# An encoder layer on one core: the two interleaved threads resume by counted TensorE time, and dense pieces hold six products

## The chip, the cores and the metric

The kernel runs on one core of a Trainium2 chip. The metric is the device time of one execution in microseconds (us). A core has a matrix engine (TensorE, PE in the rows, with its weight loads as PEld), three further engines (VectorE or DVE, ScalarE or ACT, GpSimd or POOL) and a DMA queue that SyncE (SP) issues. Each engine takes its own instructions in order and waits on semaphores for the others.

## The reference

One encoder layer over 2048 tokens of width 1024 in fp32. Three mixers run beside each other, then an output projection and a gated feed-forward layer.

```
h = rms_norm(x, norm_mix);  p = h @ w_in          # split by columns
out_a = dsa_mixer(...)   # per block of 128 queries: score all keys, keep the 256 best of the
                         # admissible ones, softmax over those, sum of latent values
out_b = gla_mixer(...)   # gated linear attention in chunks of 64, with a carried state
out_c = swa_mixer(...)   # attention in a window of 128 with sinks
x = x + concat(out_a, out_b, out_c) @ w_out
h = rms_norm(x, norm_ffn)
x = x + (silu(h @ w_ffn_gate) * (h @ w_ffn_up)) @ w_ffn_down
return rms_norm(x, final_norm)
```

## The kernel before, in words

A large product is done in fp32r as three matmuls of 512 columns for each 128 rows of the contraction (high by high, low by high, high by low halves of the operands); a weight tile that comes from memory for the first time is split into its halves on ACT (line 114) and POOL (line 117), and stored for later use.

The tokens stand in four groups of 512. The program is written by two Python generators that `merge` interleaves into one instruction stream.

- **dense** writes, for each group, `pass1` (the projections that the sparse mixer needs), then `pass2` (gated linear attention and window attention, each with their projections in `proj`), and then `ffn` for groups 0 and 1, one group at a time. The feed-forward products are lines 199 to 201 (gate and up, output projection) and 509 to 511 (down).
- **dsa** writes the sparse mixer for 16 blocks of 128 queries. `select` scores the keys (lines 1115 and 1116) and then finds the 256th best value by bisection: 8 and 23 rounds of `probe`, alternately on ACT (line 1153) and DVE (line 1155), each of which reads all keys of the block and is followed by two tiny DVE instructions that set the next threshold; then lines 1194 to 1208 make the mask, with a DVE scan (line 1203). `attend` runs for the block before, in an inner `merge` with `select`: for each head, `logits` (three matmuls, lines 1248 to 1250, for each strip of keys, reduced on DVE at line 1252, then Exp on ACT at line 1256), then for pairs of heads `turned` (four transposes at line 1265, a copy on ACT at line 1267) and `summed` (line 1275).

After each piece a generator yields its cost in us of work. `merge` divides what a thread has yielded by its total, and resumes the thread that is furthest behind. The total of dsa is multiplied by `SPEED`, 1.3; a larger number makes it count as further behind, so it is resumed earlier. `FINE`, 4, is the number of contraction tiles, of three matmuls each, after which `proj` and the feed-forward products yield, so dense comes in pieces of 12 matmuls. A thread that yields None (its input is not written yet) is passed over.

What the generators write is a program with an order of priority. The framework that builds the queues of the engines from it decides the final order on each of them, and adds all semaphores.

When both generators are at their end, `ffn` runs once more for groups 2 and 3 together (lines 352 to 354 and 509 to 511, PSUM tile `pf`). In that part one generator runs alone.

PSUM tiles for `dsa` are `sc` (2 buffers), `tr` (2, shared with dense) and `o` (1); those of dense are `mm` (2) or `mf` (3).

Of the kernel before, what the change touches and what calls it, by code (L numbers as in the profile page):

```python
# [40 lines left out]


def merge(*threads):


    live = []
    for gen, total in threads:
        live.append([0.0, float(max(total, 1e-9)), gen])
    while live:
        for t in sorted(live, key=lambda e: e[0] / e[1]):  # L50
            try:
                c = next(t[2])
            except StopIteration:
                live.remove(t)
                break
            if c is None:
                continue
            t[0] += c
            yield c
            break  # L60
        else:
            yield None

# [6 lines left out]
def drive(gen):  # L70
    for _ in gen:
        pass

SPEED = 1.3
FINE = 4

# [6 lines left out]
def hybrid_encoder_kernel(ctx, tc, xT, w_in, w_out, w_g, w_u, w_d, vec, wuk, wuv, wg2,  # L85
                          relb, cst, onehot, out):
    nc = tc.nc
    V, A, T, Q = nc.vector, nc.scalar, nc.tensor, nc.gpsimd

# [93 lines left out]
    def ffn(groups, pools, ps_f, ps_n, n_raw, n_w, n_act, n_lead, before, prepare=iter(())):  # L183
# [67 lines left out]
        def normed(i):  # L251

            hs = halves[i]
            norm_scale(hs)
            h2.append([])
            for k in range(KC):
                h2[i].append(operand(i, k))
                hi, lo = h2[i][k]
                hf = fr.tile([P, 512], F32, tag="m", bufs=n_m, name="hf")
                V.scalar_tensor_tensor(out=hf, in0=x2[:, k, hs], scalar=vc[:, V_FFN + k:V_FFN + k + 1],  # L260
                                       in1=rs[:, hs], op0=ALU.mult, op1=ALU.mult)
                A.copy(hi, hf)  # L262
                (V if k % 2 else Q).tensor_sub(lo, hf, hi.bitcast(F32))
                yield 0.4
# [302 lines left out]
    with ExitStack() as mx:  # L567
# [249 lines left out]
        def to_tokens(ps, dst):  # L817

            t = gen_tile("t")
            A.copy(t, ps)  # L820
            pt = ps_tr()
# [38 lines left out]
        def gla_qkv(j, h, bx, first=None):  # L860
            qe = gl.tile([P, 2, G], F32, tag="qe", name="qe")
            Q.memset(qe[64:128, 0, :], 0.0)
            Q.memset(qe[0:64, 1, :], 0.0)
            ke = gl.tile([P, G], F32, tag="ke", name="ke")
            kd = gl.tile([P, 4, P], F32, tag="kd", name="kd")
            vt = gl.tile([P, 2, 4, P], F32, tag="vt", name="vt")
            ps = first[0] if first else (yield from proj(CH_QB + j, h))
            for hh in range(2):
                r = slice(hh * 64, hh * 64 + 64)
                V.scalar_tensor_tensor(out=qe[r, hh, :], in0=ps[r], scalar=0.125, in1=bx["e1"][r],  # L870
                                       op0=ALU.mult, op1=ALU.mult)
            if not first:
                yield 5.2 - PART
            ps = first[1] if first else (yield from proj(CH_KB + j, h))
            db = bx["db"]
            V.tensor_mul(ke, ps, bx["e2"])
            V.tensor_mul(db, ps, db)
            pt = ps_tr()
            for t in range(4):
                T.transpose(pt[:, t * P:(t + 1) * P], db[:, t * P:(t + 1) * P], ident)  # L880
            A.copy(kd, pt.rearrange("p (b d) -> p b d", b=4))
            yield 5.7 - PART
            for hh in range(2):
                ps = yield from proj(CH_VB + 2 * j + hh, h)
                to_tokens(ps, vt[:, hh])
                yield 5.7 - PART
            bx.update(qe=qe, ke=ke, kd=kd, vt=vt)
# [15 lines left out]
        def gla_mix(g, j, bx):  # L903

            qe, ke, kd, vt, dec = (bx[n] for n in ("qe", "ke", "kd", "vt", "dec"))
            for t2 in range(2):
                pa = ps_mm()
                for u in range(2):
# [7 lines left out]
                                op=ALU.mult)  # L916
                yield 1.0

# [10 lines left out]
                for n in range(4):  # L929
# [12 lines left out]
                    S_st[j] = nw  # L942
                yield 1.8
                po = ps_ot()
# [14 lines left out]
                A.activation(sq, po, AF.Square)  # L959
                yield 1.8  # L960
                pm = ps_tr()
# [18 lines left out]
        def swa_qkv(g, h, bx):  # L980
            qc = gl.tile([P, 2, G], F32, tag="qc", name="qc")
            for i in range(2):
                ps = yield from proj(CH_QC + i, h)
                A.activation(qc[:, i, :], ps, AF.Copy, scale=0.125)
                yield 5.2 - PART
            ps = yield from proj(CH_KC, h)
            if g > 0:
                Q.tensor_copy(kct[:, 0:P], kct[:, G:G + P])
                Q.tensor_copy(vct[:, 0, :], vct[:, 4, :])
            V.tensor_copy(kct[:, P:], ps)  # L990
            yield 5.2 - PART
            ps = yield from proj(CH_VC, h)
            to_tokens(ps, vct[:, 1:5, :])
            bx["qc"] = qc
            yield 5.7 - PART

        def swa_mix(g, bx):
            qc = bx["qc"]
            for b in range(4):
# [4 lines left out]
                for kv in range(2):  # L1004
# [11 lines left out]
                    lg.append(l2)  # L1016
                yield 1.8
                den = sp.tile([P, 4], F32, tag="den", name="den")
# [10 lines left out]
                yield 1.0  # L1029
                kbs = [1] if k0 else [0, 1]  # L1030
                pts = {}
                for kb in kbs:
# [6 lines left out]
                    pts[kb] = pT  # L1039
                yield 1.2  # L1040
                po = ps_ot()
# [48 lines left out]
        def select(qb, res):  # L1090
# [18 lines left out]
            ql = selp.tile([P, 512], F32R, tag="ql", name="ql")  # L1109
            split(qf, qh, ql)  # L1110
            x = selp.tile([P, S], F32, tag="x", name="x")
            for k0, w in strips(nk):
                for hd in range(4):
                    ps = ps_sc()
                    T.matmul(ps[:, 0:w], qh[:, hd * P:(hd + 1) * P], ks[:, k0:k0 + w], start=True, stop=False)
                    T.matmul(ps[:, 0:w], ql[:, hd * P:(hd + 1) * P], ks[:, k0:k0 + w], start=False, stop=True)
                    wt = w_tok[:, qb, hd:hd + 1]
                    if hd == 0:
                        V.tensor_scalar(out=x[:, k0:k0 + w], in0=ps[:, 0:w], scalar1=0.0, scalar2=wt,
                                        op0=ALU.max, op1=ALU.mult)  # L1120
                    else:
                        r = sel_tile("r")
                        A.activation(r[:, 0:w], ps[:, 0:w], AF.Relu)
                        V.scalar_tensor_tensor(out=x[:, k0:k0 + w], in0=r[:, 0:w], scalar=wt,
                                               in1=x[:, k0:k0 + w], op0=ALU.mult, op1=ALU.add)
                yield 4 * w / 512.0
            Q.memset(x[0:64, nk - 64:nk], LOW)
# [32 lines left out]
            for i in range(8):  # L1160
# [4 lines left out]
                                op0=ALU.bitwise_or, op1=ALU.bitwise_xor)  # L1165
                yield nk / 980.0 + 0.6

# [6 lines left out]
            for k in range(1, 24):  # L1174
                lim, few, enough = probe(k % 2 == 1)
                if k < 23:
# [4 lines left out]
                                    op0=ALU.subtract, op1=ALU.add)  # L1181
                yield nk / 1000.0 + 0.6

# [7 lines left out]
            V.tensor_scalar(out=ntt, in0=ntt, scalar1=-1.0, scalar2=None, op0=ALU.mult)  # L1191
            yield nk / 960.0 + 0.8

# [15 lines left out]
            res.append(mk)  # L1209
            yield 4.0 * nk / 960.0  # L1210

# [6 lines left out]
        def attend(qb, res):  # L1218
# [3 lines left out]
            nc.sync.dma_start(out=qa[:, 0:256].rearrange("p (j t) -> p j t", j=2),  # L1222
                              in_=qaD[g].rearrange("j p t -> p j t")[:, :, q0:q0 + P])
            pq = ps_sc()
            for hd in range(4):
# [4 lines left out]
            A.activation(lh, pq, AF.Copy, scale=0.125)  # L1230
            V.scalar_tensor_tensor(out=ll, in0=pq, scalar=0.125, in1=lh.bitcast(F32), op0=ALU.mult, op1=ALU.subtract)
            x = res[0]
            nw = min(nk, 256)
# [5 lines left out]
            def logits(hd):  # L1239
# [5 lines left out]
                for si, (k0, w) in enumerate(sl):  # L1245
# [8 lines left out]
                                           op0=ALU.add, op1=ALU.min, accum_out=least[:, si:si + 1])  # L1254
                    yield 0.9 * w / 512.0
                A.activation(lg[:, 0:nk], lg[:, 0:nk], AF.Exp, scale=-1.0, bias=least[:, si:si + 1],
# [24 lines left out]
            for h2 in (0, 2):  # L1281
                yield from logits(h2)
                yield from logits(h2 + 1)
                for k4 in range(0, qb + 1, 4):
                    nxt = [turned(h2, k4)]
# [3 lines left out]
                    wait = nxt  # L1289
                    yield 2.0 * nxt[0][2] / 4.0  # L1290
            V.reciprocal(den, den)

            pt = ps_tr()
# [3 lines left out]
            summed(*wait)  # L1297
            pb = ps_tr()
            for hd in range(4):
# [167 lines left out]
```

## Time and profile before

| | us |
|---|---|
| median of 3 runs | 2904.71 (2903.05 to 2909.02) |
| the profiled execution, its own time | 2900.37 |
| its span, first to last instruction | 2898.6 |
| TensorE busy in the span | 2701.9 (93%) |
| VectorE busy | 1791.0 (62%) |
| ScalarE busy | 1251.7 (43%) |
| GpSimd busy | 837.1 (29%) |
| mean granted TensorE clock | 0.971 of full |

The span and the execution's own time differ by 1.8 us. Busy times overlap between engines, so they don't add up to the span; what matters is the idle time of the engine that sets the pace in a stage.

### The profile page before, as it was taken

To read this page: it belongs to the slowest core of one execution; us is meant where nothing else is said; L and a number is where in the kernel's file an instruction comes from. 1 tells how busy PE (TensorE), PEld (TensorE's weight loads), DVE (VectorE), ACT (ScalarE), POOL (GpSimd) and SP (SyncE) were. 2 spreads that over 40 slices of the span, in tenths; PEclk is the share of its full clock that TensorE was granted. 3 is DMA by queue.
4 is the path that set the end of the run, shared out by engine and by line. 5 is a ranking of instruction groups with operands and counts; after the bars stand their busy time and mean duration, and the time that the engine had idled before them with its cause. 6 is when DMAs were issued, how large, how long until landed. Compare 5 with 4: busy or idle time off the path is not lost. (4 is left out here: it accounts for less than half of the span.)

```text
span 2898.6 us, 37034 instructions
## 1 busy us (share of the span) xinstructions
PE 2701.9 (93%) x13108; PEld 2120.4 (73%) x13108; DVE 1791.0 (62%) x3661; ACT 1251.7 (43%) x2183; POOL 837.1 (29%) x681
## 2 busy tenths in 40 slices
PE   7898999999999989998988998999998999999997
PEld 5666767677776767776766777878776888888885
DVE  3887897787776767465477564464546544444446
ACT  4655664565555645354455342342433211111114
POOL 3113420010100454544443200000223444354443
PEclk9999999999999989999999999999999999999998
DMA  7565534243332756766667444435473443334432
GB/s 258 191 193 196 181 123 142 94 144 112 98 130 83 245 207 215 247 206 218 216 212 244 164 159 134 150 127 167 173 256 130 132 136 107 120 123 134 131 99 102
DMA packets 191113, 471.08 MB, mean 163 GB/s; under 512 B 19944, under 2 KB 51600, under 8 KB 190928
## 3 DMA queue, kind: packets, MB, share of 16 engines
q1 hardware_dynamic: 190928, 468.71, 48.8%
q8 instruction: 104, 1.70, 0.2%
q14 instruction: 81, 0.66, 0.1%
HBM read 341.61 MB, written 127.02 MB: 162 GB/s over the span
## 5 line engine op out<-in xcount | busy, mean ns | idle before, releaser
L117 POOL TENSOR_TENSOR w<-raw,w 128x512 fp32r<-128x512 f32 x272 | 366.9, 1360 | 592.5 <-ACT w L114 559.2
L1153 ACT ACTIVATE jd<-x,c 128x384 bf16<-128x384 f32 (+13 forms) x224 | 292.9, 1307 | 299.1 <-DVE c L1180 237.2
L199 PE MATMUL mf<-ah,w 128*128 128x512 f32 x832 | 333.1, 401 | 6.4 <-ACT ah L262 2.6
L201 PE MATMUL mf<-al,w 128*128 128x512 f32 x832 | 330.4, 398 | 7.8 <-DVE al L243 5.0
L1155 DVE TENSOR_SCALAR_CACHE_REDUCE jd<-x,c 128x384 bf16<-128x384 f32 (+13 forms) x224 | 330.9, 1477 | 6.9 <-DVE c L1164 0.5
L200 PE MATMUL mf<-ah,w 128*128 128x512 f32 x832 | 328.6, 396 | 0.0
L114 ACT CAST w<-raw 128x512 fp32r<-128x512 f32 x272 | 165.3, 617 | 364.3 <-PE pf L511 190.9
L354 PE MATMUL pf<-al,w 128*128 128x512 f32 x616 | 242.6, 394 | 7.4 <-DVE al L277 3.7
L352 PE MATMUL pf<-ah,w 128*128 128x512 f32 x616 | 242.4, 393 | 4.3 <-ACT ah L276 4.3
L724 PE MATMUL mm<-hh,w 128*128 128x512 f32 x576 | 240.2, 417 | 4.3 <-issue 2.0
L353 PE MATMUL pf<-ah,w 128*128 128x512 f32 x616 | 241.4, 392 | 0.0
L725 PE MATMUL mm<-hh,w 128*128 128x512 f32 x576 | 231.3, 402 | 0.0
L726 PE MATMUL mm<-hl,w 128*128 128x512 f32 x576 | 230.1, 400 | 0.0
L201 PEld LDWEIGHTS mf<-al,w 128*128 128x128 f32 x832 | 159.3, 192 | 45.0 <-DVE al L243 5.5
L199 PEld LDWEIGHTS mf<-ah,w 128*128 128x128 f32 x832 | 159.4, 192 | 40.9 <-issue 4.9
L512 DVE TENSOR_TENSOR x<-x,pf 128x512 f32<-128x512 f32 (+1 forms) x184 | 121.9, 663 | 106.1 <-PE pf L511 105.1
L200 PEld LDWEIGHTS mf<-ah,w 128*128 128x128 f32 x832 | 159.5, 192 | 32.1
L509 PE MATMUL mf<-fh,w 128*128 128x512 f32 x352 | 143.9, 409 | 17.2 <-ACT fh L114 6.9
L117 POOL TENSOR_TENSOR fl<-u,fh 128x512 fp32r<-128x512 f32 x44 | 58.0, 1319 | 320.9 <-ACT fh L114 320.9
L354 PEld LDWEIGHTS pf<-al,w 128*128 128x128 f32 x616 | 116.8, 190 | 35.3 <-DVE al L277 5.7
L510 PE MATMUL mf<-fh,w 128*128 128x512 f32 x352 | 141.4, 402 | 1.1 <-POOL w L117 1.1
L511 PE MATMUL pf<-fl,w 128*128 128x512 f32 (+1 forms) x368 | 141.2, 384 | 0.6 <-POOL fl L117 0.6
(296 smaller groups left out, 5921.9 us busy)
## 6 DMA issues: line engine op xcount, KB each, us to landing
w<-w SPq DMA_DIRECT2D x622, 512.0 KB, 3.6
raw<-in_w_g_dram SPq DMA_DIRECT2D x88, 256.0 KB, 3.6
raw<-in_w_u_dram SPq DMA_DIRECT2D x88, 256.0 KB, 3.5
xk<-in_xT_dram SPq DMA_DIRECT2D x64, 256.0 KB, 3.2
raw<-in_w_in_dram SPq DMA_DIRECT2D x44, 256.0 KB, 3.7
raw<-in_w_d_dram SPq DMA_DIRECT2D x44, 256.0 KB, 3.7
m<-mixT SPq DMA_DIRECT2D x32, 256.0 KB, 3.2
x<-in_xT_dram SPq DMA_DIRECT2D x32, 256.0 KB, 5.4
```

The costliest lines, as they stand in the source:

```text
L117: Q.tensor_sub(lo, src, hi.bitcast(F32))
L199: T.matmul(ps, a, act[k][0], start=(first and k == ks[0]), stop=False)
L200: T.matmul(ps, b, act[k][0], start=False, stop=False)
L201: T.matmul(ps, a, act[k][1], start=False, stop=(last and k == ks[-1]))
L352: T.matmul(ps, x, b[0], start=first, stop=False)
L353: T.matmul(ps, y, b[0], start=False, stop=False)
L354: T.matmul(ps, x, b[1], start=False, stop=last)
L724: T.matmul(ps, a, hh, start=(k == 0), stop=False)
L725: T.matmul(ps, b, hh, start=False, stop=False)
L726: T.matmul(ps, a, hl, start=False, stop=(k == KC - 1))
L1153: A.activation(jd, xs, AF.Sign, scale=-1.0, bias=c[:, 0:1], accum_out=cnt)
L1155: V.tensor_scalar(out=jd, in0=xs, scalar1=c[:, 0:1], scalar2=0.0, op0=ALU.is_ge, op1=ALU.add, accum_out=cnt)
```

## The change

`merge` gets a clock of its own, `now`, that `drive` advances by the TensorE time of each piece as it is written. A piece can now yield three numbers: its cost for the balance between the threads, its TensorE time, and a latency. After such a piece its thread isn't resumed until `now` has moved on by the latency; the other thread is written meanwhile. A yield of zero cost and zero TensorE time states a latency alone. When every thread waits, the shortest wait is handed up, and `drive` advances `now` by it without writing anything.

```
 def merge(*threads):
     live = []
     for gen, total in threads:
-        live.append([0.0, float(max(total, 1e-9)), gen])
+        live.append([0.0, float(max(total, 1e-9)), gen, 0.0])
     while live:
+        wait = None
         for t in sorted(live, key=lambda e: e[0] / e[1]):
+            left = t[3] - now[0]
+            if left > 1e-9:
+                wait = left if wait is None else min(wait, left)
+                continue
             ...
             if c is None:
                 continue
+            c, pe, lat = c if isinstance(c, tuple) else (c, c, 0.0)
+            if c == 0.0 and pe == 0.0:
+                t[3] = now[0] + lat
+                break
             t[0] += c
-            yield c
+            yield c, pe, 0.0
+            t[3] = now[0] + lat
             break
         else:
-            yield None
+            yield None if wait is None else (0.0, 0.0, wait)
...
-    for _ in gen:
-        pass
+    for c in gen:
+        if c is not None:
+            c, pe, lat = c if isinstance(c, tuple) else (c, c, 0.0)
+            now[0] += pe + lat
...
-SPEED = 1.3
-FINE = 4
+SPEED = 1.38
+FINE = 2
```

A yield of one number counts it as cost and as TensorE time, with no latency; the dense products stay so. The stated latencies are:

```
 # ffn, normed, ahead of norm_scale            + yield 0.0, 0.0, 4.0
 # to_tokens, between copy and transposes      + yield 0.0, 0.0, 1.2
 # gla_mix                                     1.0 -> 1.0, 0.5, 0.5
                                               1.8 -> 1.8, 0.5, 2.5
                                               1.8 -> 1.8, 1.2, 1.5
 # swa_mix                                     1.8 -> 1.8, 1.1, 0.5
                                               1.0 -> 1.0, 0.0, 5.0
                                               1.2 -> 1.2, 0.9, 2.0
 # select, after the split of the queries      + yield 0.0, 0.0, 5.0
 #   each strip: once after 4 heads            4 * w / 512.0
 #   -> after heads 2 and 4                    2 * w / 512.0, 0.9 * w / 512.0, 1.2
 #   each probe, and the mask                  cost as before, 0.0, 0.0
 # attend, after the query load                + yield 0.0, 0.0, 4.0
 #   after lh and ll                           + yield 0.4, 0.9, 3.0
 #   each strip of logits                      0.9 * w / 512.0 -> 0.9 * w / 512.0, 0.7 * w / 512.0, 1.0
 #   after the logits of two heads             + yield 0.0, 0.0, 3.5
 #   each turn of two heads                    2.0 * n / 4.0 -> 2.0 * n / 4.0, 1.6 * n / 4.0, 1.2
 #   after the reciprocal                      + yield 0.0, 0.0, 1.5
 #   after the last summed                     + yield 0.5, 0.7, 1.5
```

No instruction is added or taken away.

## Rows read from the trace of the kernel before

**Rows 1.** By stage: length; PE, PEld, DVE, ACT, POOL busy us; TensorE clock; DMA.

```profile
0.00:2077.00 2077.00, 1919.62 (x9617) 1481.41 (x9618) 1374.48 (x3096) 1048.87 (x1856) 507.05 (x439) 0.97 0.52 173
2077.00:2100.00 23.00, 19.56 (x147) 13.88 (x145) 14.87 (x29) 15.24 (x22) 6.72 (x5) 0.93 0.62 229
2100.00:2899.00 799.00, 762.75 (x3346) 625.10 (x3346) 401.69 (x538) 187.55 (x306) 323.37 (x238) 0.98 0.41 134
```

**Rows 2.** TensorE's waits from 0 to 2100 us: total us, times, longest us.

```profile
PE tr L1265 <- ACT big L1256: 21.1, 12, 7.2
PE mm L743 <- ACT hh L688: 15.4, 10, 7.2
PE sc L1248 <- DVE least L1252: 14.7, 9, 3.1
PE o L1275 <- ACT pT L1267: 7.1, 3, 6.0
PE mf L509 <- ACT fh L114: 6.9, 1, 6.9
PE tr L1300 <- DVE dT L1296: 5.4, 3, 3.1
...
PE tr L823 <- ACT t L820: 4.3, 6, 1.6
...
PE tr L1036 <- DVE l L1028: 3.6, 4, 1.9
```

**Rows 3.** VectorE around the longest of these waits, 1346 to 1354 us.

```profile
1346.35 1.69 DVE L1201 TENSOR_SCALAR mk<-jd 128x1664 bf16<-128x1664 bf16 x1
...
1349.53 3.61 DVE L1203 TENSOR_TENSOR_SCAN x<-ones,mk 128x1664 f32<-128x1664 f32 x1
1353.06 0.45 DVE L1252 CUSTOM_DVE_ANT_0 big<-sc,near,least 128x256 f32<-128x256 f32 x1
```

**Rows 4.** TensorE in the same place; in brackets its idle time before.

```profile
1355.28 1.11 PE L1265 MATMUL tr<-cs,big 128*128 128x128 f32 x4 [7.24 <-ACT big L1256]
```

**Rows 5.** TensorE where dense has ended and dsa has not.

```profile
2076.42 0.39 PE L511 MATMUL mf<-fl,w 128*128 128x512 f32 x1
...
2088.65 2.07 PE L1275 MATMUL o<-pT,cv 128*64 128x128 f32 x16
...
2092.55 1.09 PE L1275 MATMUL o<-pT,cv 128*64 128x128 f32 x16
...
2100.16 0.47 PE L199 MATMUL pf<-ah,w 128*128 128x512 f32 x1 [1.03 <-POOL al L243]
```

**Rows 6.** TensorE, from four short transposes back to dense products.

```profile
2055.77 0.60 PE L1265 MATMUL tr<-cs,big 128*128 128x128 f32 x4
2056.13 0.48 PE L509 MATMUL mf<-fh,w 128*128 128x512 f32 x1
2056.45 0.39 PE L510 MATMUL mf<-fh,w 128*128 128x512 f32 x1
2056.68 0.40 PE L511 MATMUL mf<-fl,w 128*128 128x512 f32 x1
```

**Rows 7.** Three stretches of 50 us with a low clock, columns as in Rows 1.

```profile
1000.00:1050.00 50.00, 40.62 (x181) 28.61 (x181) 38.82 (x53) 23.18 (x39) 26.00 (x18) 0.83 0.58 204
1350.00:1400.00 50.00, 44.72 (x238) 36.43 (x239) 14.83 (x20) 14.47 (x24) 19.15 (x17) 0.93 0.52 182
...
1750.00:1800.00 50.00, 43.70 (x217) 35.16 (x217) 22.33 (x32) 10.06 (x15) 3.09 (x3) 0.89 0.37 126
```

**Rows 8.** TensorE near 2042 us, where both threads have work.

```profile
2042.27 0.40 PE L199 MATMUL mf<-ah,w 128*128 128x512 f32 x1
2042.50 0.41 PE L1248 MATMUL sc<-cTh,lh 128*128 128x512 f32 x1
2042.75 0.39 PE L200 MATMUL mf<-ah,w 128*128 128x512 f32 x1
```

More of the change, by code (lines that the diff above doesn't have):

```diff
@@ L40 @@
 CH_QB, CH_KB, CH_VB, CH_RB, CH_QC, CH_KC, CH_VC, N_CH = 6, 8, 10, 14, 18, 20, 21, 22
+now = [0.0]
 def merge(*threads):
@@ L87, in hybrid_encoder_kernel @@
     nc = tc.nc
+    now[0] = 0.0
     V, A, T, Q = nc.vector, nc.scalar, nc.tensor, nc.gpsimd
@@ L253, in normed @@
             hs = halves[i]
+            yield 0.0, 0.0, 4.0
             norm_scale(hs)
@@ L820, in to_tokens @@
             A.copy(t, ps)
+            yield 0.0, 0.0, 1.2
             pt = ps_tr()
@@ L884, in gla_qkv @@
                 ps = yield from proj(CH_VB + 2 * j + hh, h)
-                to_tokens(ps, vt[:, hh])
+                yield from to_tokens(ps, vt[:, hh])
                 yield 5.7 - PART
@@ L916, in gla_mix @@
                                 op=ALU.mult)
-                yield 1.0
+                yield 1.0, 0.5, 0.5
                 pk = [ps_tr(), ps_tr()]
@@ L942, in gla_mix @@
                     S_st[j] = nw
-                yield 1.8
+                yield 1.8, 0.5, 2.5
                 po = ps_ot()
@@ L959, in gla_mix @@
                 A.activation(sq, po, AF.Square)
-                yield 1.8
+                yield 1.8, 1.2, 1.5
                 pm = ps_tr()
@@ L992, in swa_qkv @@
             ps = yield from proj(CH_VC, h)
-            to_tokens(ps, vct[:, 1:5, :])
+            yield from to_tokens(ps, vct[:, 1:5, :])
             bx["qc"] = qc
@@ L1016, in swa_mix @@
                     lg.append(l2)
-                yield 1.8
+                yield 1.8, 1.1, 0.5
                 den = sp.tile([P, 4], F32, tag="den", name="den")
@@ L1028, in swa_mix @@
                     V.tensor_scalar(out=l2, in0=l2, scalar1=den[:, hd:hd + 1], scalar2=None, op0=ALU.mult)
-                yield 1.0
+                yield 1.0, 0.0, 5.0
                 kbs = [1] if k0 else [0, 1]
@@ L1039, in swa_mix @@
                     pts[kb] = pT
-                yield 1.2
+                yield 1.2, 0.9, 2.0
                 po = ps_ot()
@@ L1110, in select @@
             split(qf, qh, ql)
+            yield 0.0, 0.0, 5.0
             x = selp.tile([P, S], F32, tag="x", name="x")
@@ L1125, in select @@
                                                in1=x[:, k0:k0 + w], op0=ALU.mult, op1=ALU.add)
-                yield 4 * w / 512.0
+                    if hd % 2:
+                        yield 2 * w / 512.0, 0.9 * w / 512.0, 1.2
             Q.memset(x[0:64, nk - 64:nk], LOW)
@@ L1165, in select @@
                                 op0=ALU.bitwise_or, op1=ALU.bitwise_xor)
-                yield nk / 980.0 + 0.6
+                yield nk / 980.0 + 0.6, 0.0, 0.0
             e0, st, ps2, up = col("e0"), col("st", F32, 32), col("ps2", F32, 32), col("up")
@@ L1181, in select @@
                                     op0=ALU.subtract, op1=ALU.add)
-                yield nk / 1000.0 + 0.6
+                yield nk / 1000.0 + 0.6, 0.0, 0.0
             V.tensor_scalar(out=up, in0=cnt, scalar1=lim, scalar2=st[:, 23:24], op0=few, op1=ALU.mult)
@@ L1191, in select @@
             V.tensor_scalar(out=ntt, in0=ntt, scalar1=-1.0, scalar2=None, op0=ALU.mult)
-            yield nk / 960.0 + 0.8
+            yield nk / 960.0 + 0.8, 0.0, 0.0
             A.activation(jd, xs, AF.Sign, scale=sg[:, 0:1], bias=ntt[:, 0:1], accum_out=cnt)
@@ L1209, in select @@
             res.append(mk)
-            yield 4.0 * nk / 960.0
+            yield 4.0 * nk / 960.0, 0.0, 0.0
         def select_cost(qb):
@@ L1223, in attend @@
                               in_=qaD[g].rearrange("j p t -> p j t")[:, :, q0:q0 + P])
+            yield 0.0, 0.0, 4.0
             pq = ps_sc()
@@ L1231, in attend @@
             V.scalar_tensor_tensor(out=ll, in0=pq, scalar=0.125, in1=lh.bitcast(F32), op0=ALU.mult, op1=ALU.subtract)
+            yield 0.4, 0.9, 3.0
             x = res[0]
@@ L1254, in logits @@
                                            op0=ALU.add, op1=ALU.min, accum_out=least[:, si:si + 1])
-                    yield 0.9 * w / 512.0
+                    yield 0.9 * w / 512.0, 0.7 * w / 512.0, 1.0
                 A.activation(lg[:, 0:nk], lg[:, 0:nk], AF.Exp, scale=-1.0, bias=least[:, si:si + 1],
@@ L1283, in attend @@
                 yield from logits(h2 + 1)
+                yield 0.0, 0.0, 3.5
                 for k4 in range(0, qb + 1, 4):
@@ L1289, in attend @@
                     wait = nxt
-                    yield 2.0 * nxt[0][2] / 4.0
+                    yield 2.0 * nxt[0][2] / 4.0, 1.6 * nxt[0][2] / 4.0, 1.2
             V.reciprocal(den, den)
+            yield 0.0, 0.0, 1.5
             pt = ps_tr()
@@ L1297, in attend @@
             summed(*wait)
+            yield 0.5, 0.7, 1.5
             pb = ps_tr()
```

## The prediction, as put on record

> **What bounds the kernel now.** I read the busy time by stage first [rows 1]. In the last stage, from 2100 us, one generator runs alone; neither the new rules nor the finer pieces can change the order of what it writes, and TensorE is busy for 762.75 of 799 us. I take this stage as fixed. In the two stretches before it, the merged part, TensorE is busy for 1919.6 + 19.6 = 1939.2 of 2100 us, VectorE for 1389.4, ScalarE for 1064.1. So TensorE sets the pace, and its 160.8 us of idle time are all that a better order could win, beside what the clock gives back.
>
> Next I read for what TensorE waits [rows 2]. The reader is to see two kinds. Some waits no new order of the two threads mends: at the start the products wait for the first scaled inputs (15.4 us for line 688), and dense waits for its own split (6.9 us for line 114). In the others, the next matmul of a dependent chain stands in the queue before its input is ready: the transposes wait for Exp (21.1 us in 12 waits), the logits for the reduction that frees their PSUM tile (14.7 in 9), the value sums for the copy (7.1 in 3), the small products of line 1300 for line 1296 (5.4 in 3), the transposes of lines 823 and 1036 (4.3 and 3.6). These are 56.2 us, and the change states a latency at each of these places.
>
> Then I looked at the longest of them. VectorE runs lines 1201 to 1203 of `select` from 1346.35 to 1353 us, the scan alone for 3.61, and only then the 0.45 us reduction that Exp needs [rows 3]; TensorE resumes at 1355.28 after 7.24 us [rows 4]. So the long wait comes from the other half of dsa, on VectorE.
>
> Last, the end of the merged part: dense's last feed-forward product starts at 2076.42, and dsa goes on until the last stage starts at 2100.16 [rows 5].
>
> **The change part by part.**
>
> *The balance, `SPEED`.* By the kernel's own costs, dense yields 1466 in all, and dsa 1322 (1024 in `select`, 298 in `attend`) against a sum of 1007.4 that `SPEED` multiplies. Before, dsa ends at 1322/(1.3 x 1007.4) = 1.010 of its total, so after dense, as the trace shows. Now `attend` yields 0.9 more for each of 16 blocks, and the ratio is 1336.6/(1.38 x 1007.4) = 0.961: dense has 0.039 x 1466 = 57 us left when dsa is written out. The last block has the most stated latency: 4 + 3, twenty strips of 1.0, two of 3.5, eight turns of 1.2 and two of 1.5, together 46.6 us, beside some 26 us of stated TensorE time of its own. Its share of the balance gives it about 34 us of dense, so it slips by 13 of the 57 and stays covered. What is won is the bare end: 23 us, of which 3.4 are idle [rows 1]; and sixteen products that took 2.07 us there took 1.09 a moment later [rows 5], another 1.0. Together 4.4; I take **4**. The price: dsa's work on VectorE and ScalarE comes 5% denser, and so do the waits that it causes dense, such as the 6.9 us of line 509 [rows 2]. If a third of the 160.8 us were of this kind, 5% of it is 2.7; I take **2**.
>
> *The stated latencies.* A dense piece is now six matmuls; in a run they start 0.23 us apart (2056.45 to 2056.68 [rows 6]), so a piece is 1.4 us. A waiting thread is held off by at least its latency, in whole pieces. From each wait [rows 2] I take off what that fills. Transposes after Exp: 3.5 us each, so the 7.2 becomes 3.7 and the other eleven go: 21.1 - 3.7 = 17.4, less some 2.2 that lie in the bare end, 15.2. Logits: one piece against nine waits with a mean of 1.6, of which the short ones save less than a piece: 9. Value sums: one piece; 6.0 becomes 4.6 and the rest goes: 2.5. Line 1300: two pieces, all but 0.4 of the longest: 5.0. Lines 823 and 1036: all, 7.9. The sum is 39.6. The bounds are 0 and 40: zero if the time that a filled gap saves is lost at the next wait, because the engine that is late gets no faster by it. I take 0.7 of it, **28**, nearer to the upper end, since only the two long ones (7.2 and 6.0) are longer than what is put in their place.
>
> *The clock.* [...] It is 0.83 from 1000 to 1050 us, where the 6.0 us wait for the copy lies, 0.93 from 1350 to 1400, behind the 7.2, and 0.89 from 1750 to 1800 [rows 7]. What is missing is worth 8.5, 3.5 and 5.5 us, 17.5 together. Two of these waits stay in part (4.6 and 3.7 us), so I take **6**; the bounds are 0 and 17.5. [...]
>
> *The finer pieces and new yields.* They add no instruction, but more changes between short and long matmuls. After four short transposes the second dense product starts 0.32 us after the first, against 0.23 in a run [rows 6]: 0.09 us a change. The new yields are six in each of 16 attends, 38 in `select` and 20 in `to_tokens`, at most some 154 changes, 14 us; many fall where the order changed already, or leave the order as it was. I take a third, **5**. The issues of DMAs move with their pieces and keep their order within a thread; the dense weights are issued by dense alone, and only the small query loads of dsa change place among them.
>
> **The sum.** 4 - 2 + 28 + 6 - 5 = 31 us. The profiled execution took 2900.4 us, so 2869; the median of the runs is 4.3 above that execution, and for the median the forecast is **2874**.
>
> **The rivals.**
>
> *Nothing to win (0.12).* A logits matmul stands between the first and the second of three dense matmuls that the program writes without a yield between them [rows 8]. So the queue isn't in the written order: the framework has moved up what it held to be ready. Then it already does what the new rule is to do; what is left is what it judged wrongly, and another order of priority meets the same errors elsewhere. The time stays within 2899 to 2910. Against it: the 7.24 us wait is just such an error, and a stated latency moves the transposes back behind dense. [...]
>
> *Slower by late evictions (0.15).* While `attend` waits, `select` is the ready half of dsa, and its probes state no TensorE time and no latency, so more of them are written together ahead of dense's evictions on VectorE and ScalarE. The place is the feed-forward part of the merge, where 88 gate and up products need both engines before line 509 can run. The mask's run of nearly 7 us [rows 3] is the sort of thing that they then stand behind, 3.6 us for the scan alone. If 12 more evictions stand behind such a scan, 43 us, the gains of 38 are gone with the costs of 7 still to pay: +12, 2917. It decides from nine on (31/3.6). For it: line 509 already waited 6.9 us once. Against it: the balance still weighs each probe by its cost.
>
> *dsa late at the end in spite of `SPEED` (0.05).* If the latencies pile up so that the last attend is written after dense, most of its 46.6 us of latencies stand bare, some 30 us more than the bare end now: 2915 to 2935.
>
> *All of it (0.15).* Every stated latency hits, the small waits that I left out too, and the clock comes back: 4 - 2 + 40 + 17.5 and no cost of changes, 60 us and a little more: 2838 to 2857.
>
> **How the numbers follow.** The forecast has 0.50 for 2857 to 2890, and a smaller gain than that, up to 2899, 0.03. The range of eight in ten goes from 2840 to 2917: it takes in most of the full gain, the case without effect, and the slower one up to its price. A measurement of this kernel tells about 0.2%, 6 us, from no change. Faster by more than that: 0.50 + 0.03 + 0.15 = 0.68; within it: 0.12; slower: 0.15 + 0.05 = 0.20.
>
> **What would show it.** In the new profile the wait of line 1265 for line 1256 falls from 21.1 to about 6 us, and that of line 1248 from 14.7 to about 6; no stretch is left in which dsa runs without dense ahead of the last stage; that stage starts near 2069 us and lasts as long as before. I am wrong if lines 509 and 199 wait longer than before for VectorE and ScalarE, if the last stage changes its length, or if the idle time of TensorE only gets other names.

## The result: slower by 1.1%, lost in the two passes

| | before | after |
|---|---|---|
| median, us (range) | 2904.86 (2903.05 to 2909.02) | 2935.74 (2929.9 to 2939.57) |
| ratio after to before, 95% interval | | 1.0106 (1.0092 to 1.012) |
| profiled execution, us | 2900.37 | 2939.57 |
| granted TensorE clock, whole span | 0.971 | 0.965 |

The forecast was 2874 with a range of 2840 to 2917; the time lies outside it. The profiled execution after is the slowest of its four, so its 39 us over the one before split a little more than the 31 us between the medians.

The first reading is the one by stage. I cut at three events in TensorE's order: the first feed-forward product (the end of passes 1 and 2), dense's last product, and the first product of the last stage. After:

```profile
0.00:1018.00 1018.00, 909.45 (x4633) 670.44 (x4634) 744.49 (x1960) 575.42 (x1157) 186.74 (x185) 0.95 0.45 146
1018.00:2124.00 1106.00, 1043.21 (x5104) 829.29 (x5102) 634.85 (x1155) 483.07 (x711) 331.03 (x255) 0.98 0.56 190
2124.00:2132.00 8.00, 3.48 (x30) 1.98 (x29) 2.94 (x5) 5.77 (x8) 0.81 (x1) 0.96 0.50 197
2132.00:2938.00 806.00, 766.52 (x3346) 627.16 (x3345) 409.71 (x543) 188.59 (x308) 329.75 (x242) 0.97 0.43 137
```

The kernel before, cut at the same events (its other two stretches stand in [rows 1]; the bare end is cut at 2077 there, so it is 23 us and not 24):

```profile
0.00:972.00 972.00, 888.47 (x4603) 655.91 (x4603) 730.82 (x1927) 561.14 (x1139) 182.12 (x182) 0.98 0.47 151
972.00:2076.00 1104.00, 1030.15 (x5010) 824.67 (x5011) 642.66 (x1169) 487.52 (x718) 324.93 (x257) 0.96 0.56 192
```

The reader is to see four differences: the passes take 46 us more, the merged feed-forward part 2 more, the bare end 16 less, the last stage 7 more. Of the 46, TensorE is idle 25 us longer (108.6 against 83.5) and busy 21 us longer at nearly the same number of products, at a clock of 0.95 instead of 0.98.

The waits of TensorE from 0 to 2140 us (total, times, longest), with the names of [rows 2]; lines have moved by 20 to 25, so 1265, 1256, 1248, 1252, 509 are 1290, 1281, 1273, 1277, 529:

```profile
PE sc L1273 <- DVE x L1141: 12.9, 3, 9.5
...
PE mf L529 <- DVE u L512: 9.6, 4, 3.4
PE sc L1273 <- DVE least L1277: 9.4, 6, 3.4
...
PE tr L1290 <- ACT big L1281: 2.4, 3, 1.7
```

The wait of the transposes for Exp has fallen from 21.1 to 2.4 us, more than forecast, and that of the logits from 14.7 to 9.4. In their place the logits now wait 12.9 us for line 1141, the first term of `select`'s scores on VectorE, once for 9.5 us.

Then I looked for where the 46 us lie. TensorE's order at the end of the second pass:

```profile
983.57 0.39 PE L746 MATMUL mm<-hl,w 128*128 128x512 f32 x1
...
990.94 1.03 PE L931 MATMUL mm<-qe,ke 128*128 128x256 f32 x4
...
1001.51 2.12 PE L1290 MATMUL tr<-cs,big 128*128 128x128 f32 x8 [1.66 <-DVE st L961]
...
1004.83 0.80 PE L970 MATMUL ot<-att,vt 128*128 128x128 f32 x2 [0.59 <-DVE att L934]
...
1016.85 0.44 PE L1290 MATMUL tr<-cs,big 128*128 128x128 f32 x2 [2.30 <-ACT pT L1292]
...
1017.58 0.50 PE L218 MATMUL mf<-ah,w 128*128 128x512 f32 x1
```

From 983.57 to 1017.58 there is no projection and no feed-forward product: only the short products of the mixers (lines 931 to 983) and of dsa. The kernel before has such a stretch at the same place, but a shorter and denser one. By windows, before, and then two of after:

```profile
949.00:972.00 23.00, 20.62 (x147) 14.79 (x145) 19.76 (x47) 19.06 (x34) 12.42 (x9) 1.00 0.77 262
```

```profile
431.00:464.00 33.00, 19.99 (x98) 14.66 (x98) 23.37 (x59) 12.71 (x24) 6.13 (x7) 0.66 0.19 61
984.00:1018.00 34.00, 27.84 (x172) 20.78 (x172) 27.97 (x66) 27.54 (x47) 15.73 (x12) 0.85 0.67 228
```

From 431 to 464 us, too, TensorE gets only products of dsa and of the gated mixer; it is idle for 13 us of 33, and the mean clock is 0.66. Of the 13 us, 9.48 are the long wait of the logits from above; line 1141 comes behind the mask of `select` (lines 1224 to 1231) on VectorE:

```profile
439.51 0.56 DVE L1231 TENSOR_TENSOR mk<-mk,jd 128x768 bf16<-128x768 bf16 x1
439.99 0.75 DVE L1141 TENSOR_SCALAR x<-sc,w_tok 128x512 f32<-128x512 f32 x1
```

```profile
440.79 0.80 PE L1273 MATMUL sc<-cTh,lh 128*128 128x512 f32 x1 [9.48 <-DVE x L1141]
```

I call a projection (`mm<-hh` or `mm<-hl`) or a feed-forward product (`mf`) a dense product. In TensorE's order the stretches of more than 6 us from one of them to the next sum to 105 us in the passes before, and to 162 after; in the merged feed-forward part they fall from 55 to 31.

Last, the entry to the last stage, after:

```profile
2123.87 0.40 PE L531 MATMUL mf<-fl,w 128*128 128x512 f32 x1
2124.20 1.09 PE L1300 MATMUL o<-pT,cv 128*64 128x128 f32 x16
2126.52 1.10 PE L252 MATMUL tr<-rs,ones 128*128 128x512 f32 x2 [1.23 <-DVE rs L247]
...
2128.10 0.65 PE L1328 MATMUL tr<-dT,cs 4*64 4x128 f32 x8 [0.37 <-DVE dT L1323]
2131.67 0.79 PE L218 MATMUL pf<-ah,w 128*128 128x512 f32 x1 [2.92 <-ACT ah L261]
```

dsa now ends with dense, as forecast [rows 5], but the last stage's first norm and its split stand between, 2.92 us for line 261 alone.

### The profile page after: what moved, and what is told of

The parts are those of the page before. It is cut to its first block, busy times and chain, and to the rows that moved or that the text cites. A ratio compares the mean times of both kernels' runs of the same rounds, so it can differ in the third digit from the quotient of the medians.

```text
span 2937.8 us, 37015 instructions
## 1 busy us (share of the span) xinstructions
PE 2722.7 (93%) x13108; PEld 2128.9 (72%) x13108; DVE 1792.0 (61%) x3661; ACT 1252.8 (43%) x2183; POOL 848.3 (29%) x681
## 4 chain that ended last, share of the span: by engine, by line
PE 44%; DVE 7%; issue 5%; ACT 2%; DMA 2%; POOL 2%; SPq 0%; DVEq 0%; ACTq 0%; POOLq 0%
PE pf L374 5%; PE pf L373 5%; PE pf L372 5%; PE mf L220 4%; PE mf L218 4%; PE mf L219 4%; DVE jd L1178 3%; PE pf L531 3%; PE pf L530 3%; PE pf L529 3%; PE mf L531 2%; PE mf L530 2%; PE mf L529 2%; ACT jd L1176 1%; PE o L1300 1%
## 5 line engine op out<-in xcount | busy, mean ns | idle before, releaser
L531 PE MATMUL mf<-fl,w 128*128 128x512 f32 x352 | 141.7, 403 | 1.3 <-POOL fl L136 1.3
```

Source lines behind the costliest of these rows:

```text
L531: T.matmul(ps, hi[:, os_], al[:, hs], start=False, stop=(j == n - 1))
```

## The experiments

The expectations name theories by letters. A: the stated latencies cost the time in the passes (E: those of the mixers, which hold dense back where there is nothing to put beside it; F: those of dsa). B: the finer pieces cost it. C and H: the balance (`SPEED`) does. G: a cost that dense loses with `FINE`. D: any other order costs about as much. Every kernel here computes the whole layer. "Parts" below are, from the profile: passes / merged feed-forward part / bare end / last stage; before 972 / 1104 / 24 / 799, after 1018 / 1106 / 8 / 806. Ratios are to the kernel before, with 95% intervals. The parts come from one execution each and are known only to some 10 us: e7 and e16 below give the four engines the same instructions in the same order throughout the passes, and yet these took 964 and 974 us, at a clock of 0.98 and 0.96.

**Each part of the change undone.** `SPEED` back:

```diff
-SPEED = 1.38
+SPEED = 1.3
```

> The changed kernel with SPEED back at 1.3; the latencies and the pieces of six stay. Theory A (the stated latencies cost the time in the second pass, by holding a chain back until it meets the long VectorE runs of select): 2925 to 2945, and the bare end of dsa comes back, since dsa's total is 1.02 of its share. Theory B (the pieces of six cost it, by changing between the threads twice as often): the same. Theory C (dsa pressed forward by 5% takes VectorE and ScalarE from the mixers in the second pass): 2900 to 2915, and TensorE's idle time from 270 us to the first feed-forward product falls from 63 to about 40 us.

2940.65 us, 1.0129 (1.0113 to 1.0145); 996 / 1078 / 65 / 801. The bare end is 65 us long. So this kernel needs about 1.38 for its two threads to end together.

The finer pieces back:

```diff
-FINE = 2
+FINE = 4
```

> The changed kernel with FINE back at 4, so dense pieces of 12 matmuls; the latencies and SPEED 1.38 stay. Theory A: 2925 to 2945, since the latencies are still there. Theory B: 2895 to 2910, and the number of changes between dense and other matmuls falls back to that of before. Theory C: 2925 to 2945.

2934.29 us, 1.0096 (1.0075 to 1.0116); 994 / 1115 / 8 / 805, from a profiled execution that is 11 us below the median. No difference from after in the total.

The finer pieces alone, in the kernel before:

```diff
-FINE = 4
+FINE = 2
```

> The kernel before with FINE 2 alone, so dense pieces of six matmuls and nothing else. Theory A: 2900 to 2910, as before. Theory B: 2925 to 2945, all of the loss. Theory C: 2900 to 2910.

2934.3 us, 1.0101 (1.0084 to 1.0119); 992 / 1091 / 53 / 798: this one edit costs as much as the whole change. The bare end shows a part of it:

```profile
2083.00:2136.00 53.00, 41.20 (x272) 29.99 (x271) 24.00 (x54) 25.70 (x37) 9.50 (x9) 0.87 0.27 100
```

It has grown from 24 to 53 us, and together with the feed-forward part it is 16 us longer (1144 against 1128). `FINE` stands in a cost too: after each of its 16 leads, `ffn` yields `3.9 - 0.65 * (KC - FINE)` (`KC` is 8), which is 1.3 with 4 and 0 with 2, though the lead's product has yielded 2.6 either way; and `gla_qkv` yields `5.7 - PART` for a product already made, 3.1 with 4 and 1.8 with 2, four times. Dense loses 20 x 1.3 = 26 us of its 1466 in counted cost, not in work, and so dsa is resumed too late. The larger part, 20 us, lies in the passes, at a clock of 0.95 instead of 0.98; why, these runs don't show.

All latencies to zero, in the changed kernel:

```diff
             c, pe, lat = c if isinstance(c, tuple) else (c, c, 0.0)
+            lat = 0.0
```

> The changed kernel with every stated latency taken as 0; the new places at which the threads yield, the pieces of six and SPEED 1.38 stay. Theory A: 2895 to 2910; the first feed-forward product starts near 972 us as before, not at 1018. Theory B and theory C: 2925 to 2945.

2931.82 us, 1.0095 (1.0079 to 1.0112); 988 / 1120 / 9 / 804. The total hardly moves (-4), against theory A, but its parts do. By the two profiled executions, which lie 17 us apart, the latencies cost 30 us in the passes (1018 - 988) and win 14 in the feed-forward part (1120 - 1106). But undoing the balance or the pieces shortens the passes too, by 22 (e1) and 24 us (e2), so these edits alone don't say which part of the change costs them.

The latencies of one half of them. First those of the mixers and of `to_tokens` to zero (`yield 1.0, 0.0, 5.0` to `yield 1.0, 0.0, 0.0` and so on), those of dsa kept:

> The changed kernel with the latencies of the two mixers and of to_tokens at 0; those of dsa and of normed stay. Theory E (in the second pass the mixers' latencies, 30 us in a window mixer beside 34 us of dense and 9 us in a gated mixer beside 2 us, hold dense itself, and TensorE has only dsa): the first feed-forward product starts near 975 to 990 us, not 1018, and the time is 2895 to 2915. Theory F (it is dsa's latencies that cost the second pass): it starts near 1015 and the time is 2925 to 2945. Theory D (the kernel before is a favourable order, and any other order costs about 1%): 2920 to 2940 whatever stays.

2933.84 us, 1.0092 (1.0075 to 1.0108); 1009 / 1109 / 8 / 804. Then those of `select` and `attend` to zero, the mixers' kept:

> The changed kernel with the latencies of dsa (select and attend) at 0; those of the mixers, to_tokens and normed stay. Theory E: the first feed-forward product starts near 1010 us or later and the time is 2930 to 2950. Theory F: it starts near 985 and the time is 2900 to 2915. Theory D: 2920 to 2940.

2937.11 us, 1.0112 (1.0096 to 1.0128); 1006 / 1114 / 9 / 804. Each takes about 10 us from the passes, neither changes the total: inconclusive, with the lost cost and 1.38 still in both.

**The lost cost held apart.** `FINE` 2 in the kernel before, with the costs as they were:

```diff
-FINE = 4
+FINE = 2
-                yield 3.9 - 0.65 * (KC - FINE)
+                yield 1.3
-            yield 5.7 - PART
+            yield 3.1 if first else 5.7 - PART
```

> The kernel before with FINE 2 and two yields corrected, so that the output projection and the first products of the gated mixer count what they counted before (with FINE 2 they lose 26 of dense's 1466). Theory G (FINE 2 alone costs 30 us because dense counts for less, and so dsa ends later: 53 us of dsa without dense instead of 24): the bare end is back at 20 to 30 us and the time at 2900 to 2912. Theory B (the pieces of six themselves): 2925 to 2940 with a bare end near 24. Theory D: 2920 to 2940.

2897.7 us, 0.9975 (0.9965 to 0.9985), with the bare end back at 23 us:

```profile
0.00:964.00 964.00, 880.28 (x4607) 652.12 (x4607) 738.95 (x1935) 565.96 (x1145) 181.38 (x183) 0.98 0.48 154
964.00:2072.00 1108.00, 1029.45 (x5008) 824.73 (x5009) 640.00 (x1162) 484.62 (x712) 325.32 (x256) 0.97 0.56 190
2072.00:2095.00 23.00, 19.96 (x148) 14.31 (x147) 14.88 (x29) 14.85 (x22) 6.33 (x5) 0.93 0.62 229
```

So with the costs kept the finer pieces don't slow the kernel (the gain of 0.25% is less than orders scatter, below), and what hurt in e3 comes with the lost cost.

The balance alone, in the kernel before, just so far that the bare end goes:

```diff
-SPEED = 1.3
+SPEED = 1.32
```

> The kernel before with SPEED 1.32 alone, so dsa ends at 0.994 of its total and some 8 us of dense are left. Theory G, that the bare end is worth what stands in it: 2885 to 2900. Its rival, that the last stage's loads and splits then stand bare in place of dsa: 2898 to 2908, with the last stage some 6 us longer. Theory D: 2920 to 2940, since the order is another one.

2921.67 us, 1.0056 (1.0033 to 1.008).

```profile
0.00:993.00 993.00, 900.42 (x4613) 663.42 (x4613) 742.02 (x1945) 566.85 (x1147) 181.33 (x183) 0.96 0.46 149
993.00:2111.00 1118.00, 1042.43 (x5146) 831.66 (x5145) 644.31 (x1172) 494.12 (x729) 327.70 (x257) 0.97 0.56 191
2111.00:2119.00 8.00, 2.30 (x7) 0.84 (x5) 4.06 (x7) 6.18 (x8) 0.00 (x0) 0.82 0.85 305
```

```profile
2111.65 0.39 PE L511 MATMUL mf<-fl,w 128*128 128x512 f32 x1
2115.28 1.26 PE L233 MATMUL tr<-rs,ones 128*128 128x512 f32 x2 [3.24 <-DVE rs L228]
2119.19 0.76 PE L199 MATMUL pf<-ah,w 128*128 128x512 f32 x1 [2.65 <-DMA w<-w]
```

The bare end is gone, and with it nothing is won: its products are now in the feed-forward part (+14 us), and the last stage's norm and weight load, which dsa's end used to cover, stand bare for 8 us. The passes grew by 21 us though nothing in them had changed but the order.

Two more balances for e7's kernel, 1.28 and 1.38 in place of 1.3:

> The kernel before with pieces of six and the costs kept, and SPEED 1.28, so dsa ends at 1.025 of its total, 20 us more of it after dense. Theory H (a balance further to dsa costs, one further from it only moves dsa's work behind dense): 2905 to 2915, all of the difference to 2898 after the last dense product. Theory D (an order other than the tuned one costs up to 1% wherever it falls): 2898 to 2930, with a loss in the first two passes.

2928.49 us, 1.008 (1.0068 to 1.0093); 974 / 1101 / 54 / 797.

> The kernel before with pieces of six and the costs kept, and SPEED 1.38: the change without its latencies and without the lost costs. Dsa ends at 0.951 of its total. Theory H: 2920 to 2935; no dsa is left after dense, and the first two passes and the feed-forward part together take up all that is won there and more. If the balance is harmless and the latencies are to blame (theory A): 2895 to 2905.

2914.12 us, 1.0034 (1.0022 to 1.0047); 996 / 1105 / 13 / 804. Here, without any latency, the feed-forward part and the bare end together take 1118 us, 13 less than e7's 1131, and the last stage 3 more. And 1.305, to see how far the order alone scatters:

> Pieces of six with the costs kept and SPEED 1.305: a change of 0.4% in the balance, to see how much an order moves the time by itself. Theory H and theory A: 2893 to 2903, with the first feed-forward product at 960 to 970 us. Theory D: the two passes move by 10 to 30 us, the time 2905 to 2930.

2913.05 us, 1.0027 (1.0014 to 1.0039); 986 / 1111 / 21 / 798. A change of the balance by 0.4% costs 15 us; the passes alone grew by 22. None of the three is better than 1.3.

**The latencies at a held balance.** The changed kernel with e7's costs and a `SPEED` that makes up for the costs added in `attend`:

```diff
-SPEED = 1.38
+SPEED = 1.314
-                yield 3.9 - 0.65 * (KC - FINE)
+                yield 1.3
-            yield 5.7 - PART
+            yield 3.1 if first else 5.7 - PART
```

> The changed kernel with dense's costs counted as before in pieces of six, and SPEED 1.314, so that dsa ends at 1.010 of its total as in the kernel before: what is left of the change is the pieces of six and the stated latencies. Theory H (the loss is the balance: SPEED and the lost costs; the latencies come out at about zero): 2893 to 2908. Theory A (the latencies cost, in the second pass): 2918 to 2935, with the first feed-forward product after 990 us against 964 in the kernel with pieces of six alone.

2943.98 us, 1.0127 (1.0111 to 1.0143); 1011 / 1094 / 42 / 796. It differs from e7 by the latencies and new yields, and is 46 us slower, more than either theory had expected. The loss is in the passes, but the two late stretches gain nothing either, 1136 us against e7's 1131, though the wait for Exp has fallen from 24.7 to 4.8 us:

```profile
1011.00:2105.00 1094.00, 1018.62 (x4923) 817.19 (x4923) 636.66 (x1160) 480.65 (x705) 318.83 (x254) 0.96 0.56 192
2105.00:2147.00 42.00, 33.88 (x243) 25.61 (x242) 19.14 (x40) 22.88 (x34) 9.41 (x7) 0.88 0.35 126
```

Then the dose, all latencies by one factor (in `drive` and in the wait that is handed up, too):

```diff
-                t[3] = now[0] + lat
+                t[3] = now[0] + lat * LAT
-            t[3] = now[0] + lat
+            t[3] = now[0] + lat * LAT
+LAT = 0.5
```

> The kernel with pieces of six, latencies, costs kept and SPEED 1.314, with every stated latency halved. Theory A (the loss in the two passes grows with the latency; the first feed-forward product starts at 1011 us with the latencies whole, near 979 with none): it starts near 995, and the time is 2915 to 2930. Theory D (any other order loses as much): it starts anywhere from 965 to 1015, without regard to the size of the latency.

2933.99 us, 1.01 (1.0087 to 1.0113). With `LAT = 2.0`:

> The same kernel with every stated latency doubled. Theory A: the first feed-forward product starts near 1040 us and the time is 2960 to 2990. Theory D: it starts anywhere from 965 to 1015, the time 2900 to 2945.

2971.22 us, 1.0222 (1.0202 to 1.0242). And latencies from the feed-forward part on only (`late[0]` is set to 1 when the second pass of all groups is written; `SPEED` 1.3, the two costs added in `attend` 0):

```diff
-            t[3] = now[0] + lat
+            t[3] = now[0] + lat * late[0]
```

> Pieces of six with the costs kept and SPEED 1.3; the stated latencies count only from the end of the second pass on, so beside the feed-forward products, and the two added costs in attend are 0. Theory A in its narrow form (the latencies cost in the second pass and gain in the feed-forward part, where TensorE's idle time fell from 75 to 63 us): 2880 to 2892. If they gain nothing there either: 2895 to 2902.

2899.92 us, 0.9982 (0.9973 to 0.9991); 979 / 1079 / 42 / 797. The total is in the range expected without a gain; but the passes are 15 us longer than e7's, and the two late stretches 10 us shorter. The four doses in one view, the first feed-forward product (shortest, median and longest duration, first and last start), for none in the passes (e12), half (e13), whole (e9) and double (e14), then the passes of e12, e9 and e14 by windows:

```profile
L218 PE MATMUL mf<-ah,w x832: 387/389/795, 979.3 to 2041.1; 128*128 128x512 f32 x167
```

```profile
L219 PE MATMUL mf<-ah,w x832: 386/390/793, 997.5 to 2080.0; 128*128 128x512 f32 x167
```

```profile
L218 PE MATMUL mf<-ah,w x832: 387/389/794, 1010.7 to 2087.7; 128*128 128x512 f32 x167
```

```profile
L219 PE MATMUL mf<-ah,w x832: 386/390/797, 1041.7 to 2116.8; 128*128 128x512 f32 x167
```

```profile
0.00:979.00 979.00, 893.48 (x4607) 656.32 (x4607) 740.47 (x1935) 566.84 (x1145) 185.21 (x183) 0.97 0.47 151
```

```profile
0.00:1011.00 1011.00, 914.51 (x4600) 674.39 (x4601) 732.97 (x1927) 563.73 (x1141) 183.83 (x185) 0.94 0.46 148
```

```profile
0.00:1042.00 1042.00, 929.93 (x4618) 684.79 (x4619) 725.33 (x1915) 562.83 (x1140) 183.18 (x185) 0.92 0.44 143
980.00:1042.00 62.00, 50.82 (x273) 35.39 (x272) 48.47 (x117) 44.37 (x80) 19.36 (x16) 0.83 0.43 140
```

The passes end at 979, 998, 1011 and 1042: the more latency, the later. The stretches without a dense product in the passes sum to 124, 163, 160 and 249 us. From e12 to e9, for the same products, TensorE is busy 21 us longer and idle 11 us longer; the larger part is busy time, at a granted clock of 0.94 instead of 0.97. The double dose leaves 62 us without a dense product in one piece.

Whose latencies? In e9's kernel, those of the gated mixer to zero, then those of both mixers and of `to_tokens`:

> The kernel with pieces of six, latencies, costs kept and SPEED 1.314 (2944 us, first feed-forward product at 1011), with the three latencies of the gated mixer at 0. Theory E (its tail stands beside 2 us of dense or beside nothing, so 4.5 us of latency for each half and 9 for a group hold dense itself): up to 4 x 9 = 36 us less, the first feed-forward product at 980 to 990, and the last stretch without a dense product, 41 us from 969, falls below 30. Theory F (dsa's latencies cost the passes): it stays above 1000.

2936.21 us, 1.0109 (1.0083 to 1.0135); 1006 / 1087 / 42 / 799.

> The same with all latencies of the two mixers and of to_tokens at 0, so that in the two passes only dsa's are left. Theory E: 975 to 990 for the first feed-forward product, 2900 to 2915 in all. Theory F: above 1000 and 2930 to 2945, as with all of them.

2921.39 us, 1.0071 (1.0044 to 1.0099); 989 / 1093 / 41 / 798. Of the 32 us between e9 and e12 in the passes, 22 go with the latencies of the mixers and of `to_tokens`, 10 with dsa's. Only 5 go with the gated mixer's, where theory E had expected 20 to 30. The stretches without a dense product stay at 161 us in e15 (160 in e9) and fall to 111 in e18.

**A version that beats both.** e12 without the new yields in the passes, where their latency is zero but they still cut the pieces differently:

```diff
-            yield 0.0, 0.0, 1.2
+            if late[0]:
+                yield 0.0, 0.0, 1.2
```

and so at each of the new yields.

> Pieces of six, costs kept, SPEED 1.3, and the latencies with their new yields only from the end of the second pass on; the two passes are written exactly as in the kernel with pieces of six alone. If the latencies help beside the feed-forward products, as theory A's narrow form has it: the first feed-forward product at 964 us, the part from there to the last stage about 10 us shorter than its 1131, 2882 to 2892. If that gain is lost in a longer bare end of dsa: 2893 to 2902.

2885.28 us (2879.61 to 2892.89), 0.9933 (0.9919 to 0.9948).

```profile
0.00:974.00 974.00, 893.71 (x4607) 664.33 (x4607) 739.64 (x1935) 566.46 (x1145) 180.89 (x183) 0.96 0.47 153
974.00:2052.00 1078.00, 1018.67 (x4917) 817.08 (x4918) 637.18 (x1152) 474.87 (x703) 326.51 (x255) 0.97 0.57 195
2052.00:2092.00 40.00, 32.96 (x240) 23.46 (x238) 18.88 (x39) 22.27 (x34) 9.09 (x7) 0.91 0.35 132
```

Against e7, the feed-forward part and the bare end together are 1118 us instead of 1131, and TensorE's idle time in them falls from 82 to 66. The passes are the same in both, so in this pair of orders the latencies are worth 13 us beside feed-forward products; e9 against e7 is a pair in which they are worth nothing there.

## Why the prediction was wrong

The step that failed is *the stated latencies*: +28 was forecast, and at a held balance they cost 46 us (e9 against e7); in the changed kernel itself they win nothing (without them it is 4 us faster, e4).

- I read the waits that a latency could fill and took for granted that the other thread always has something long to fill them with, and that a filled wait is won. The wait for Exp did fall with the dose, 24.7 us without latencies (e7), 12.0 with half (e13), 4.8 with the whole (e9) and 4.0 with double (e14), while the kernel got slower each time. Beside feed-forward products some orders gained: the two late stretches took 1114 us after against 1128 before, and 1118 in e16 against 1131 in e7. But they took 1136 in e9, and e11 reached 1118 without a latency. I had taken 28, so the term was at least twice too large even there.
- In the second pass the latencies stand in dense itself. The window mixer states 0.5 + 5 + 2 = 7.5 us for each of its four blocks, 30 in all, and an inner `merge` sets beside it projections with a stated 33.6 us; the second gated mixer of a group states 2 x (0.5 + 2.5 + 1.5) = 9 us, beside 2.1 us of the next group's work, and beside nothing in the last group. When that partner has run out, dense is held, and TensorE gets only the short, dependent products of dsa and the mixers; from 431 to 464 us it was idle for 13 us of them, and the clock was 0.66. That the latencies in the passes cost time is shown by the dose, e12 and e18. That it comes by partners that run out is read from the stretches without dense products (160 us in e9, 111 in e18), and no run gave a partner more work. For the gated mixer e15 doesn't bear it out; the window mixer and `to_tokens` were not taken apart. My sum had the mixers' latencies only as a gain (7.9 us for lines 823 and 1036) and never as time in which dense is held, and of the 56.2 us of waits that it fills only 16 lie in the passes.
- *The clock* (+6) had the wrong sign: of the 46 us that the passes grew, 21 are longer busy time at 0.95 instead of 0.98. In the feed-forward part the clock did rise, from 0.96 to 0.98. No run shows the 6 us: that shorter waits keep the clock up was my estimate, and while the wait for Exp fell from 21.1 to 2.4 us, the clock of the whole span went from 0.971 to 0.965.
- *The balance* (+4 - 2): the bare end fell from 24 to 8 us as forecast, but that wins nothing. By e8 the work of dsa there moves into the feed-forward part (+14) and the last stage's norm and loads lose their cover; the last stage began at 2132, not 2069, and became 7 us longer, where I had taken it as fixed.
- Also there, I overlooked that `FINE` changes dense's counted cost. Without the 26 us dense ends at 1440/1466 = 0.982 of its total, not at 1, and has 0.021 x 1466 = 31 us left when dsa is written out at 0.961, not 57. e3 shows what comes with the lost cost by itself (37 us against e7), and e1 that 1.38 makes up for the bare end (65 us at 1.3, 8 at 1.38) but for only 5 us of the total.
- *The finer pieces* (-5): no such cost was seen. In TensorE's order the changes between dense and other products fell from 929 before to 893 in e7, and with the costs kept the finer pieces gained 7 us (e7), which is within the scatter of orders.

Of the rivals, none named the passes. "Slower by late evictions" had the right sign at a price of 12 us instead of 31, but its place, the feed-forward part, stayed within 2 us (1104 to 1106), and the waits of lines 509 and 199 for VectorE and ScalarE went only from 23 to 25 us. "dsa late at the end" came nearest in its number, 2915 to 2935, but dsa ended with dense. "Nothing to win" was right that filled gaps are partly lost again, as the 12.9 us wait for line 1141 shows. Two of my three signs of being wrong came: the last stage changed its length, and idle time got other names.

What stays open: the losses don't add. Removing all latencies from the changed kernel gives back 4 us in the median (e4, 17 between the profiled executions), so they alone don't explain its 31 us. Removing them from the passes of e9's gives 44 (e12), of which 32 are in the passes and 15 in the feed-forward part. Of these 15, some 5 lie where e9 has one wait that e12 lacks, at the first norm of that part, for which the profile names no releaser:

```profile
1069.48 2.04 PE L252 MATMUL tr<-rs,ones 128*128 128x512 f32 x2 [12.25 <-issue]
```

For the rest I have no cause. Without any latency the passes took from 964 to 996 us for small changes of order (e7, e17, e8, e11), mostly by longer busy time at a lower granted clock: 880 us at 0.98 in e7, 899 at 0.96 in e17, 900 at 0.96 in e8, 907 at 0.95 in e11. Why one order keeps the clock up and a neighbouring one does not, or one execution and another of the same order (e7, e16), these runs don't show. A difference of 15 us between two orders can be of this kind; the steady course of the dose over 63 us can hardly be. The gain of e16 over e7, 12 us, is within that scatter.

## What to carry to other kernels

A stated latency can help only where the other thread has independent work at that moment, and a wait that it fills is not yet time won; before stating one, add up the latencies of a stage and the partner's work in the same stage, for each thread. When a constant sets both the size of the pieces and their counted cost, change one at a time, and look at where the threads end. An interleaving whose time scatters by 0.5% for a 0.4% change of a weight has to be compared by stages and by dose, not by one pair of totals.

## What the runs showed of the hardware that was not expected

The clock fell without a long wait. In the changed kernel, by windows of 4 us:

```profile
452.00:456.00 4.00, 3.24 (x27) 1.67 (x28) 2.02 (x6) 3.88 (x8) 0.57 (x1) 1.00 0.00 0
456.00:460.00 4.00, 2.56 (x21) 2.11 (x19) 3.87 (x12) 1.88 (x4) 1.97 (x2) 0.86 0.10 32
460.00:464.00 4.00, 4.00 (x20) 4.00 (x20) 1.39 (x8) 0.00 (x0) 0.00 (x0) 0.50 0.11 34
```

From 452 to 460 us TensorE is busy for 5.80 of 8 us, after two products of 512 columns only with products of 64 and 128, the longest wait among them 0.97 us; from 460 to 464 it is busy without a break, at a granted clock of 0.50. My prediction had looked for low clocks behind long waits only; here the clock fell, to 0.86 and then 0.50, behind waits of under 1 us.

The price of such a stretch is seen on equal products of the changed kernel, the two of line 970: 0.44 us at 993.61, and 0.80 at 1004.83, above. The granted clock around them is 1.00 and 0.50:

```profile
993.61 0.44 PE L970 MATMUL ot<-att,vt 128*128 128x128 f32 x2
```

```profile
990.00:995.00 5.00, 4.71 (x35) 4.16 (x34) 5.00 (x18) 4.61 (x7) 2.89 (x3) 1.00 0.62 193
1003.00:1010.00 7.00, 6.41 (x29) 5.68 (x28) 5.38 (x10) 3.83 (x7) 4.04 (x3) 0.50 0.74 267
```
